# First-layer seams of a two-layer trunk: order of gates, inputs, a table load and roundings

## Chip, cores and metric

The kernel runs on one core of a Trainium2 chip. The metric is the device time of one execution in microseconds; three runs of the kernel before took 2288.21, 2284.48 and 2288.95 us (median 2288.21). A separate profiled execution gave the trace.

## What is computed

A decoder trunk of two layers over 528 tokens (16 learned meta tokens and 512 of the input), width 1024, all in float32. Each layer adds half a SwiGLU block, a mixer, and half a second SwiGLU block, each on an RMS-normalised input. Layer 0 mixes with an RWKV-7 recurrence, layer 1 with sparse attention:

```python
h = h + 0.5 * swiglu(rms_norm(h, g[0]), w_in[i, 0], w_out[i, 0])
hn = rms_norm(h, g[1])
# layer 0: six mixes of hn and its shift by one token
xx = shift(hn) - hn
xr, xw, xk, xv, xa, xg = hn + xx * mix[0..5]
r, k, v = xr @ w_r, xk @ w_k, xv @ w_v
w_log = -softplus(-(w0 + tanh(xw @ w1) @ w2)) - 0.5
a = sigmoid(a0 + (xa @ a1) @ a2)
g = sigmoid(xg @ g1) @ g2
# scan over tokens, normalisation, bonus ...
h = h + ((yn + bonus) * g) @ w_o
h = h + 0.5 * swiglu(rms_norm(h, g[2]), w_in[i, 1], w_out[i, 1])
```

The SwiGLU blocks have a hidden width of 2816.

## The kernel before, in words

**Matmuls.** Activations lie transposed, features on the 128 partitions and tokens along the free dimension, and all work is done for two ranges of tokens, A (0 to 272) and B (272 to 528). Every float32 operand of a large product is split into a rounded high part and a remainder, so that a block of weights (128x128) takes three matmuls: high by high, high by low, low by high (`mm3`). The weights come in units of 128x1024 over one DMA queue (SP); ACT rounds a unit to its high part (tile `whi`), DVE subtracts for the low part (`wlo`). `Weights.take` hands out blocks in a fixed order and, with each, has the units rounded that lie two or three ahead. `Weights.prefetch` asks for the same earlier.

**Stages of the first layer.** Feed-forward on A; projections on A; feed-forward on B, with the scan of A beside it; output projection of A, at the end of which the projections on B begin (`joined`, L1489); second feed-forward on A, with the scan of B beside it; output projection of B. The rest is the second layer and what remains of the first.

**Projections (`proj`, L882).** The normalised input and its difference to the shifted input are made per 128 features. `queue` (L917) lists 48 mixes, six of eight tiles, in the order in which they are needed. `mix` (L898) computes a mix on DVE into a tile `tb` (four buffers), takes a pair of high and low tiles from a pool of 14 (`pairs`; tile `p`) and makes a closure `make` (L906) that rounds the high part on ACT and subtracts the low part on POOL. `late` holds the closure back until the next mix has been issued; when the queue is empty it runs at once. `need` (L934) issues mixes or closures until an operand is there; `done` gives pairs back and `mixes` spends them.

`proj_steps` (L83) lists the steps: dense projections with `wk`, `wv`, `wr` in two halves of four output tiles each (kind "d"), the two low-rank first products (kind "lora", keys `lw` and `la`; `lw` ends with a tanh), the low-rank second products (kind "wa2", `decay`, L972: two banks, evacuated with a sigmoid into tile `gm`), the powers (kinds "E" and "P": exp, then sigmoid) and the eight steps of the gate's first product (`g1`). The dense results are evacuated by ACT into `BKV` and `AR`. After `g1` the gates' sigmoid goes into `R.sg` (L1042).

**Inputs of the next feed-forward.** `ahead` (L1485) first calls `norm.stat`, which does nothing when the range's rstd is there, and then walks `norm.steps` (L651): nine steps, each with an apply on DVE (into a `tb`), and, one step behind, a rounding on ACT and a subtraction on DVE into a pair. `proj` advances it once in each of the last six `g1` steps (L1038); what is left runs as the feed-forward starts.

**Statistics.** `Norm.stat` (L612) sums squares over partitions with matmuls on a tile of ones, runs eleven small DVE operations (`newton`: tile `nst`), and returns `spread` (L631), which multiplies by the identity to bring rstd to all partitions. `early` (L828) issues the statistics at item `at` of a running stage, and `spread` at an item above `at + apart`, once the planner's clock has the newton done.

**PSUM.** Four banks `acc` for large products, three `bg` for everything else, one `ry` for the scan, and for the product of `lw` (L562, L565).

**Output projection (`outproj`, L1398).** For each of eight tiles, `gate` (L1405) makes the gate's second product in a `bg` bank; DVE combines it with the scan's result, then the pair is split. Three output tiles run along with the gates (items 0 to 10 of the stage), five follow with eight items each.

**Order of work.** Each engine's order is written out by the program: a planner with a clock of modelled costs (`Clock`, `run`) weaves the chains beside the main stage. ACT, DVE and POOL run their instructions in that order.

Of the kernel before, what the change touches and what calls it, by code (L numbers as in the profile page):

```python
# [13 lines left out]
AF = mybir.ActivationFunctionType  # L14
# [10 lines left out]
A = (0, 272)  # L25
B = (272, 528)
# [12 lines left out]
NG, MIX, W0, A0, KK, KA, RK, LNG, LNB = 0, 48, 96, 104, 112, 120, 128, 136, 144  # L39
# [466 lines left out]
def trunk(ctx, tc, wall, plan, h0, vec, cstd, gqk, out, stop=None, gap=0.0, share=400.0, slack=200.0, fulls={}):  # L506
    clock = Clock()
    nc = Core(tc.nc, clock)
# [47 lines left out]
    up, down = small[:, 0:1], small[:, 1:2]  # L556
# [8 lines left out]
    def bbank(tag="bg"):  # L565
        return psum.tile([128, 512], F32, name=tag, bufs={"bg": 3, "ry": 1}[tag])
# [21 lines left out]
    class Norm:  # L588


        def __init__(self, i):
            self.gcol = NG + 8 * i
            self.ss, self.last, self.rstd = {}, {}, {}

        def add(self, d, r, lag=None):
# [16 lines left out]
        def stat(self, r, keep=True):  # L612


            if r in self.rstd:
                return None
            n = r[1] - r[0]
            q = 68 if n == 272 else 128
            nq = n // q
            p = bbank()  # L620
            for i, src in enumerate((self.ss[r], self.last[r])):
                for j in range(nq):
                    nc.tensor.matmul(p[:q, j:j + 1], src[:, j * q:j * q + q], ones[:, 0:1],
                                     start=i == j == 0, stop=i == 1, skip_group_check=True)
            st = work.tile([128, 3, 4], F32, name="nst", bufs=1)
            it = work.tile([128, 4], I32, name="nsti", bufs=1)
            x, y, a = (st[:q, j, :nq] for j in range(3))
            nc.vector.tensor_scalar(x, p[:q, :nq], EPS, None, op0=OP.add)
            newton(y, x, it[:q, :nq], a)

            def spread():  # L631
                p = bbank()
                for j in range(nq):
                    nc.tensor.matmul(p[:, j * q:j * q + q], y[:, j:j + 1].to_broadcast([q, 128]), ident[:q, :q],
                                     start=True, stop=True)
                self.rstd[r] = p
                if keep:
                    self.rstd[r] = work.tile([128, 272], F32, name="rstd", bufs=2)
                    nc.scalar.activation(self.rstd[r][:, :n], p[:, :n], AF.Copy)

            if keep:
                return spread
            W.prefetch(3 if "again" in W.kind[W.flat[W.pos][0]:W.flat[W.pos][0] + 1] else 0)
            spread()
# [183 lines left out]
    def early(main, norm, r, at=12, X=None, start=0, every=4, apart=0):  # L828


        steps = spread = None
        due = 10 ** 6
        own = Chain(None)

        def mine(f, *a):
            clock.chain = own
            x = f(*a)
            clock.chain = None
            return x

        for i, c in enumerate(main):
            if i == at:
                spread = mine(norm.stat, r)
            elif i > at + apart and spread and own.ready + gap < clock.t["tensor"]:
                spread = mine(spread)
                due = i + 3
            if X and i >= start and i > at and not spread and (own.ready - 800 <= clock.t["tensor"] or i >= due):
                steps = steps or norm.steps(X(), r)
                mine(next, steps, None)
                due = i + every  # L850
            yield c
        if spread:
            spread()
        if X:
            steps = steps or norm.steps(X(), r)
            for _ in steps:
                pass
# [24 lines left out]
    def proj(R, norm, pairs, core, ahead):  # L882
# [13 lines left out]
        xm, slot, late = {}, {}, []  # L896

        def mix(i, d):  # L898

            x = work.tile([128, 288], F32, name="tb", bufs=4)  # L900
            nc.vector.scalar_tensor_tensor(x[:, :n], xx[d // 4][:, d % 4, :n], col(MIX + 8 * i + d),
                                           hn[d][:, 1:1 + n], op0=OP.mult, op1=OP.add)
            slot[i, d] = pairs.take()
            hi, lo = (slot[i, d][1][:, j, :n] for j in range(2))

            def make():  # L906
                nc.scalar.activation(hi, x[:, :n], AF.Copy)
                nc.gpsimd.tensor_tensor(lo, x[:, :n], hi.bitcast(F32), op=OP.subtract)
                xm[i, d] = hi, lo

            if late:
                late.pop()()
            late.append(make)
            if not queue:
                late.pop()()

        queue = [(i, d) for i in (2, 1, 4, 3, 0, 5) for d in range(DT)]  # L917

        def done(i, *ds):
            for d in ds:  # L920
                pairs.give(slot.pop((i, d)))

        def mixes(k):
            while k and queue and pairs.free:
                i, d = queue.pop(0)
                if i == 2:
                    norm.apply(d, r, hn[d][:, 1:1 + n])
                    nc.vector.tensor_sub(xx[d // 4][:, d % 4, :n], hn[d][:, 0:n], hn[d][:, 1:1 + n])
                mix(i, d)
                if i == 2 and pad and d % 4 == 3:  # L930
                    nc.scalar.activation(hnlast[:, d - 3:d + 1], hn2[d // 4][:, :, n:n + 1], AF.Copy)
                k -= 1

        def need(i, d):  # L934
            while (i, d) not in xm:
                if pairs.free and queue:
                    mixes(1)
                else:
                    late.pop()()
            return xm[i, d]  # L940

        R.AR = core.tile([128, DT, 9, 2, CH], F32, name="AR")
# [2 lines left out]
        R.P = pa_[:, 0].rearrange("p m (c t) -> p m c t", t=33)  # L945
        R.a = pa_[:, 1]
        R.sg = core.tile([128, 2, 288], F32, name="sg")
        nc.gpsimd.memset(R.P[:, :, :, 0:1], 0.0)
        lslot = pairs.take()
        xw, xa = (lslot[1][:, j, :n] for j in range(2))  # L950
# [45 lines left out]
        for kind, *st in proj_steps():  # L996
            if kind == "d":
                key, g, ds = st
                if ds[0] == 0:
                    ps = [bank() for _ in range(4)]  # L1000
                x = [need(mixof[key], d) for d in ds]
                mixes(len(ds))
                for m, p in enumerate(ps, 4 * g):
                    for d in ds:
                        w = W.take(blk(key, d, m))
                        yield p[:, :n], *w, *x[d - ds[0]]
                        mm3(p[:, :n], w, x[d - ds[0]], d == 0, d == DT - 1)
                    if ds[-1] == DT - 1:
                        evac(key, m, p[:, :n])
                if g:  # L1010
                    done(mixof[key], *ds)
                    mixes(len(ds))
                yield
            elif kind == "lora":
                key, d = st
                if d == 0:
                    pl = key, bbank("ry" if key == "lw" else "bg")
                mm3(pl[1][:, :n], W.take(blk(key, d, 0)), need(mixof[key], d), d == 0, d == DT - 1)
                done(mixof[key], d)
                mixes(1)  # L1020
                if d == DT - 1:
                    lora_end(*pl)
                yield
            elif kind == "wa2":
                decay(st[0])
                if st[0] == DT - 1:
                    pairs.give(lslot)
                yield
            elif kind in "EP":
                powers(kind, st[0])  # L1030
            else:
                d = st[0]
                pg = pg or (bank(), bank())
                x = need(5, d)
                for m in range(2):
                    mm3(pg[m][:, :n], W.take(blk("g1", d, m)), x, d == 0, d == DT - 1)
                done(5, d)
                if d >= 2:  # L1038
                    next(ahead)
                if d == DT - 1:  # L1040
                    for i, k in ((0, 128), (1, 64)):
                        nc.scalar.activation(R.sg[:k, i, :n], pg[i][:k, :n], AF.Sigmoid)  # L1042
                yield
        R.have.add("all")

# [404 lines left out]
            end(m, p)  # L1450


    norms = [Norm(i) for i in range(6)]

    def first(main):

# [32 lines left out]
    def joined():  # L1489

        main = proj(RB, norms[1], pairs, core, stepsA)
        for i, c in enumerate(early(outproj(RA, pairs, norms[2]), norms[1], B, at=6, apart=4)):
            if i in (27, 31, 35):
                assert B in norms[1].rstd
                next(main)
            yield c
        yield from early(main, norms[2], A, at=100, apart=16)
# [37 lines left out]
        for _ in steps:  # L1535
            pass

    run(early(first_x(outproj(RB, pairs, norms[2], after)), norms[3], A, at=6, apart=4))
    right.close()
    xq = xa[0]  # L1540

# [456 lines left out]
```

## Time and profile before

| | |
|---|---|
| Runs | 2284.48, 2288.21, 2288.95 us |
| Profiled execution | 2284.38 us, span 2282.5 us |
| PE busy | 2217.5 us |
| DVE busy | 1662.1 us |
| ACT busy | 1274.8 us |
| POOL busy | 159.4 us |
| Mean granted PE clock | 0.995 of full |

PE is TensorE's matmuls, PEld its weight loads, DVE VectorE, ACT ScalarE, POOL GpSimd. A row of the timeline gives start and length in us, engine, line, operation, output and inputs by tile name, shape and count; the bracket behind it gives how long the engine had been idle and whose work ended that. All instructions carry line L385, that of the helper which records them, so rows are told apart by tile names: `p` are pairs (mixes, inputs, hidden tiles), `tb` the values before rounding, `gm` the decays, `sg` the gates, `nst` the statistics, `AR` and `BKV` the projections' results.

### The profile page before, as it was taken

What the parts mean: (1) busy time and instruction counts of PE and PEld (TensorE: products, weight loads), DVE (VectorE), ACT (ScalarE), POOL (GpSimd) and SP (SyncE); (2) the same over time, 40 slices, a digit from 0 to 9 for tenths busy, and PEclk for the clock granted to TensorE, in tenths of its full rate; (3) what the DMA queues carried; (4) which work ended last, traced back from release to release, by engine and by line L of the source; (5) the groups of instructions that cost most, each with busy time, mean ns of one, the idle gap of its engine ahead of it and who ended that gap; (6) DMA issues with size and microseconds to landing.
All of it is one profiled execution on the core that took longest, in us unless ns stands there. A gap on an engine that the chain in (4) does not pass through costs nothing.

```text
span 2282.5 us, 49521 instructions
## 1 busy us (share of the span) xinstructions
PE 2217.5 (97%) x20058; PEld 2151.9 (94%) x20058; DVE 1662.1 (73%) x3247; ACT 1274.8 (56%) x2186; POOL 159.4 (7%) x228
## 2 busy tenths in 40 slices
PE   8998999999999999999999999999999999999999
PEld 8998999999888999999999999899998899989999
DVE  7677777767777975686566658887657998866665
ACT  6454784475567545655444545458744657675443
POOL 0000522010052010010000000000000000000000
PEclk9999999999999999999999999999999999999999
DMA  8887757522684554255455554453454453434654
GB/s 298 282 295 253 237 200 238 188 71 86 201 306 149 172 162 130 72 190 197 166 184 165 188 171 156 166 182 133 148 178 156 158 180 117 156 104 151 190 185 139
DMA packets 115030, 405.17 MB, mean 178 GB/s; under 512 B 13024, under 2 KB 17200, under 8 KB 114800
## 3 DMA queue, kind: packets, MB, share of 16 engines
q1 hardware_dynamic: 112592, 397.07, 51.9%
q0 software_dynamic: 2208, 4.92, 0.9%
q8 instruction: 158, 2.59, 0.5%
q14 instruction: 72, 0.59, 0.1%
HBM read 380.88 MB, written 21.05 MB: 176 GB/s over the span
## 4 chain that ended last, share of the span: by engine, by line
PE 81%; DVE 9%; ACT 5%; issue 3%; DMA 1%; POOL 1%; SPq 0%; ACTq 0%; DVEq 0%; POOLq 0%
PE acc L385 69%; PE bg L385 8%; PE ry L385 4%; DVE wlo L385 3%; ACT whi L385 2%; DVE tb L385 1%; DMA wraw<-wall 1%; POOL p L385 1%; ACT p L385 1%; DVE rel L385 1%; DVE h L385 0%; ACT gm L385 0%; DVE m L385 0%; DVE pr L385 0%; ACT L385 0%
## 5 line engine op out<-in xcount | busy, mean ns | idle before, releaser
L385 ACT ACTIVATE whi<-wraw 128x1024 fp32r<-128x1024 f32 (+2 forms) x674 | 705.2, 1052 | 412.4 <-PE acc L385 247.7
L385 DVE TENSOR_TENSOR wlo<-wraw,whi 128x1024 fp32r<-128x1024 f32 (+3 forms) x628 | 767.1, 1225 | 172.0 <-ACT whi L385 162.5
L385 PE MATMUL acc<-p,whi 128*128 128x272 f32 (+1 forms) x4192 | 806.4, 291 | 24.4 <-ACT whi L385 6.2
L385 PEld LDWEIGHTS acc<-p,whi 128*128 128x128 f32 x4192 | 658.7, 190 | 34.3 <-ACT p L385 7.0
L385 PE MATMUL acc<-p,wlo 128*128 128x272 f32 (+1 forms) x2096 | 603.0, 288 | 0.4 <-DMA wlo<-lo 0.2
L385 PEld LDWEIGHTS acc<-p,wlo 128*128 128x128 f32 x2096 | 398.3, 190 | 1.1 <-DVE wlo L385 0.7
L385 PE MATMUL acc<-xa_hi,whi 128*128 128x256 f32 (+1 forms) x1088 | 311.1, 286 | 1.6 <-DVE h L385 1.6
L385 PE MATMUL acc<-xa_hi,wlo 128*128 128x256 f32 (+1 forms) x1088 | 309.4, 284 | 2.8 <-DVE wlo L385 2.7
L385 PE MATMUL acc<-xa_lo,whi 128*128 128x256 f32 (+1 forms) x1088 | 308.6, 284 | 0.0
L385 PE MATMUL acc<-hid_hi,whi 128*128 128x256 f32 (+1 forms) x880 | 252.4, 287 | 4.6 <-DVE h L385 3.4
L385 PE MATMUL acc<-hid_lo,whi 128*128 128x256 f32 (+1 forms) x880 | 248.9, 283 | 0.4 <-DVE hid_lo L385 0.4
L385 PE MATMUL acc<-hid_hi,wlo 128*128 128x256 f32 (+1 forms) x880 | 249.1, 283 | 0.0
L385 PE MATMUL acc<-xb_hi,whi 128*128 128x256 f32 x752 | 214.2, 285 | 0.0
L385 PE MATMUL acc<-xb_hi,wlo 128*128 128x256 f32 x752 | 211.4, 281 | 0.0
L385 PE MATMUL acc<-xb_lo,whi 128*128 128x256 f32 x752 | 211.4, 281 | 0.0
L385 PEld LDWEIGHTS acc<-xa_hi,wlo 128*128 128x128 f32 x1088 | 206.1, 189 | 3.9 <-DVE wlo L385 3.9
L385 PEld LDWEIGHTS acc<-xa_hi,whi 128*128 128x128 f32 x1088 | 206.2, 189 | 3.0 <-DVE h L385 1.8
L385 PEld LDWEIGHTS acc<-xa_lo,whi 128*128 128x128 f32 x1088 | 206.3, 190 | 0.0
L385 PEld LDWEIGHTS acc<-hid_hi,whi 128*128 128x128 f32 x880 | 165.8, 188 | 7.3 <-issue 4.3
L385 PEld LDWEIGHTS acc<-hid_lo,whi 128*128 128x128 f32 x880 | 166.9, 190 | 0.7 <-DVE hid_lo L385 0.6
L385 PEld LDWEIGHTS acc<-hid_hi,wlo 128*128 128x128 f32 x880 | 166.2, 189 | 0.0
L385 DVE SCALAR_TENSOR_TENSOR h<-acc,h 128x256 f32<-128x256 f32 (+1 forms) x288 | 117.0, 426 | 58.8 <-PE acc L385 58.4
(283 smaller groups left out, 3205.2 us busy)
## 6 DMA issues: line engine op xcount, KB each, us to landing
wraw<-wall SPq DMA_DIRECT2D x659, 512.0 KB, 3.6
wlo<-lo SPq DMA_DIRECT2D x46, 512.0 KB, 4.9
lo<-wlo SPq DMA_DIRECT2D x32, 512.0 KB, 4.1
wraw<-wall SPq DMA_DIRECT2D x10, 438.0 KB, 3.4
out<-h SPq DMA_DIRECT2D x8, 256.0 KB, 2.5
h<-h SPq DMA_DIRECT2D x2, 512.0 KB, 8.0
ynat<-L POOLq DMA_DIRECT2D x2, 512.0 KB, 3.8
T<-ynat POOLq DMA_DIRECT2D x2, 512.0 KB, 3.7
```

Source lines behind the costliest of these rows:

```text
L385: r = f(*args, **kw)
```

## The change

1. In the last `g1` step the two gate sigmoids are issued before the pairs are given back and before the next input step.
2. `ahead` is advanced after each step of a second half of a dense projection as soon as the queue of mixes is empty and a pair is free, and in each `g1` step when a pair is free.
3. `late` becomes first in, first out, and holds two closures instead of one; when the queue is empty all are run.
4. A sigmoid of one element is issued before the first mix of each range's projections.
5. The statistics and their spread of the norm before the second feed-forward (`norms[2]`) take the `ry` bank in place of `bg`.
6. In both output projections `early` issues the statistics at item 9 instead of 6.

```diff
-        def __init__(self, i):
-            self.gcol = NG + 8 * i
+        def __init__(self, i, tag="bg"):
+            self.gcol, self.tag = NG + 8 * i, tag
...
-            p = bbank()
+            p = bbank(self.tag)
...
-                p = bbank()
+                p = bbank(self.tag)
...
-            if late:
-                late.pop()()
             late.append(make)
-            if not queue:
-                late.pop()()
+            while len(late) > (2 if queue else 0):
+                late.pop(0)()
...
-                    late.pop()()
+                    late.pop(0)()
...
         R.sg = core.tile([128, 2, 288], F32, name="sg")
+        nc.scalar.activation(R.sg[:, 0, 0:1], down, AF.Sigmoid)
...
                     done(mixof[key], *ds)
                     mixes(len(ds))
+                    if not queue and pairs.free:
+                        next(ahead)
...
-                done(5, d)
-                if d >= 2:
-                    next(ahead)
                 if d == DT - 1:
                     for i, k in ((0, 128), (1, 64)):
                         nc.scalar.activation(R.sg[:k, i, :n], pg[i][:k, :n], AF.Sigmoid)
+                done(5, d)
+                if pairs.free:
+                    next(ahead, None)
...
-    norms = [Norm(i) for i in range(6)]
+    norms = [Norm(i, "ry" if i == 2 else "bg") for i in range(6)]
...
-        for i, c in enumerate(early(outproj(RA, pairs, norms[2]), norms[1], B, at=6, apart=4)):
+        for i, c in enumerate(early(outproj(RA, pairs, norms[2]), norms[1], B, at=9, apart=4)):
...
-    run(early(first_x(outproj(RB, pairs, norms[2], after)), norms[3], A, at=6, apart=4))
+    run(early(first_x(outproj(RB, pairs, norms[2], after)), norms[3], A, at=9, apart=4))
```

## Prediction

> **What bounds the kernel now.** I read the page first, then the time by stage, then the waits of PE in order of time, and last the rows of ACT and DVE around each wait.
>
> ```profile
> span 2282.5 us, 49521 instructions
> PE 2217.5 (97%) x20058; PEld 2151.9 (94%) x20058; DVE 1662.1 (73%) x3247; ACT 1274.8 (56%) x2186; POOL 159.4 (7%) x228
> ```
>
> PE is busy for all but 65.0 us of the span. The change adds and removes no matmul, so the only time to be had is PE's idle time, and time in which PE runs slowly. The windows below are the projections of the two ranges (212 to 326 and 636 to 740), the two output projections (597 to 636 and 1010 to 1046), and all that comes after the first layer's seams. Columns: stretch, length, busy us of PE, PEld, DVE, ACT and POOL (instructions), granted PE clock, DMA share, GB/s.
>
> ```profile
> 212.00:326.00 114.00, 101.39 (x788) 99.30 (x788) 86.73 (x137) 80.94 (x188) 47.65 (x50) 0.96 0.60 202
> ...
> 597.00:636.00 39.00, 33.32 (x257) 32.15 (x256) 30.30 (x72) 17.68 (x31) 1.67 (x2) 1.00 0.64 227
> 636.00:740.00 104.00, 95.02 (x762) 92.72 (x761) 78.57 (x124) 74.91 (x149) 42.63 (x48) 0.97 0.61 217
> ...
> 1010.00:1046.00 36.00, 32.84 (x275) 31.87 (x274) 26.61 (x67) 19.91 (x39) 0.11 (x1) 1.00 0.65 235
> 1046.00:2282.50 1236.50, 1213.47 (x9714) 1173.14 (x9713) 878.16 (x1783) 670.59 (x1086) 0.10 (x1) 1.00 0.49 161
> ```
>
> In the four stages PE idles 12.6, 5.7, 9.0 and 3.2 us: 30.5 us out of 293, against 23.0 us in the 1236 us that follow. No other engine is full there (DVE and ACT are at 71 to 78% of the projections), so these are waits in a chain, not a second bound. The timeline of PE names the waits that the change can touch; the bracket is the idle time and what ended it.
>
> ```profile
> 256.58 0.52 PE L385 MATMUL acc<-p,whi 128*128 128x272 f32 x2 [1.59 <-ACT BKV L385]
> ...
> 290.39 0.52 PE L385 MATMUL acc<-p,whi 128*128 128x272 f32 x2 [1.11 <-ACT BKV L385]
> ...
> 326.14 0.39 PE L385 MATMUL acc<-p,whi 128*128 128x256 f32 x1 [2.44 <-ACT sg L385]
> ...
> 609.50 0.36 PE L385 MATMUL bg<-p,whi 128*128 128x272 f32 x1 [1.47 <-DVE tb L385]
> ...
> 616.19 0.39 PE L385 MATMUL acc<-p,whi 128*128 128x272 f32 x1 [2.43 <-ACT p L385]
> ...
> 667.13 0.39 PE L385 MATMUL acc<-p,whi 128*128 128x256 f32 x1 [1.38 <-ACT BKV L385]
> ...
> 680.31 0.48 PE L385 MATMUL bg<-ident,nst 68*128 68x68 f32 x1 [2.46 <-ACT gm L385]
> ...
> 697.95 0.39 PE L385 MATMUL bg<-p,whi 128*128 128x256 f32 x1 [2.17 <-ACT gm L385]
> ...
> 740.87 0.40 PE L385 MATMUL acc<-p,whi 128*128 128x272 f32 x1 [2.38 <-ACT sg L385]
> ...
> 1025.95 0.39 PE L385 MATMUL acc<-p,whi 128*128 128x256 f32 x1 [0.89 <-ACT p L385]
> ```
>
> These ten make 18.3 us. Two of them are followed by a stretch in which the granted clock is a half:
>
> ```profile
> 679.69:686.52 6.83, 6.21 (x30) 6.21 (x30) 1.82 (x2) 1.57 (x5) 0.00 (x0) 0.50 0.22 77
> 741.13:744.54 3.41, 3.41 (x17) 3.41 (x17) 3.20 (x7) 2.66 (x5) 0.00 (x0) 0.50 0.00 0
> 613.76:616.19 2.43, 0.00 (x1) 0.00 (x1) 1.69 (x11) 0.48 (x2) 0.00 (x0) 1.00 1.01 325
> ...
> 299.00:318.70 19.70, 19.70 (x160) 19.70 (x159) 11.60 (x14) 19.60 (x42) 3.96 (x5) 1.00 0.48 162
> ```
>
> An equal wait at 613.76 to 616.19 did not lower it. So a wait of 2.4 us costs the clock sometimes, by where it falls.
>
> **The change part by part.**
>
> *Gate sigmoids first.* Two activations (per range) move ahead of one input step. At the end of the first projection ACT does this:
>
> ```profile
> 323.84 0.42 ACT L385 ACTIVATE p<-tb 128x256 fp32r<-128x256 f32 x1 [1.63 <-DVE tb L385]
> 324.16 1.04 ACT L385 ACTIVATE whi<-wraw 128x1024 fp32r<-128x1024 f32 x1
> 325.11 0.71 ACT L385 ACTIVATE p<-tb 128x256 fp32r<-128x256 f32 x2
> 325.72 0.65 ACT L385 ACTIVATE sg<-acc 128x272 f32<-128x272 f32 x2
> ```
>
> PE's last g1 matmul ends at 323.70 (326.14 less 2.44); the gates start 2.0 us later because three roundings of inputs and one of weights stand ahead, the first of them itself waiting 1.63 for DVE. With the inputs gone from there the gates start when PE is done. PE has two free banks to go on with, so little of the 0.65 shows; a weight rounding of 1.04 can still stand ahead. I leave 0.3 of each wait (bounds 0 and 1.0): 2.44 + 2.38 - 0.6 = 4.2 saved (2.8 to 4.8). If the wait at 740.87 goes, so should the half clock behind it: 3.41 us at a half is 1.7 (0 to 1.7).
>
> *Inputs from the last dense projection on.* The same eight applies, eight roundings and eight subtractions per range, with no statistics in them, since both ranges' rstd exist by then, and no transfer moved: the two prefetch calls ask for units that the matmuls have asked for already. Following the lists of free pairs through the steps, the queue of mixes is empty after the first `wr` step of the second half; five `wr` steps and four `g1` steps then issue all nine input steps, where before six came in `g1` and the rest after it. What is queued behind: each rounding waits for PE to have read the pair that it overwrites, and the weight roundings stand behind it on ACT. ACT has 0.10 idle in 299 to 318.7, while PE has none, so PE lives off weights rounded ahead. Four roundings of 0.42 fall into the `wr` steps, 1.7 us; the idle time just after (the 1.63 above is a part) takes them in. Cost between 0 and 1.7 per projection; I take 0.5 each, 1.0.
>
> *Sigmoid table early, statistics in the other bank.* The load exists already; it moves.
>
> ```profile
> 678.49 1.28 ACT L385 ACT_TABLE_LOAD   x1
> 679.78 0.84 ACT L385 ACTIVATE gm<-bg,vecs 128x256 f32<-128x256 f32 x2
> ...
> 219.84 0.43 ACT L385 ACTIVATE p<-tb 128x272 fp32r<-128x272 f32 x1 [6.21 <-DVE tb L385]
> 221.66 0.43 ACT L385 ACTIVATE p<-tb 128x272 fp32r<-128x272 f32 x1 [1.39 <-DVE tb L385]
> ...
> 629.06 0.42 ACT L385 ACTIVATE p<-tb 128x256 fp32r<-128x256 f32 x1 [2.21 <-DVE tb L385]
> ```
>
> Its new places are ACT's waits of 6.21 and 2.21: hidden, with the one-element activation behind it (0.43 at most, the nearest row). If that cover were gone it would cost 1.3. The next activation starts 1.29 after the load, so 1.29 is what a load costs ACT here. The Trainium skill ("ScalarE: Activation LUTs", What ACT_TABLE_LOAD costs) puts a drain of about 1.38 us on top; this trace shows none; by that rule each moved load would free 1.4 us more.
>
> At 680.31 the spread of the statistics waits for a `bg` bank that a decay's sigmoid frees. In its own `ry` bank, last read at the lora's end, well before, it waits for nothing: 2.46 saved. The spread itself takes less at full clock, as the same shape does later:
>
> ```profile
> 680.31 1.98 PE L385 MATMUL bg<-ident,nst 68*128 68x68 f32 x8 [2.46 <-ACT gm L385]
> ...
> 1027.81 1.01 PE L385 MATMUL bg<-ident,nst 68*128 68x68 f32 x8
> ```
>
> That is 0.97; and from 682.29 to 686.52 PE runs at a half, 2.1. Sum 5.5 (2.46 if the half clock comes anyway).
>
> A rule of the Trainium skill speaks against the clock terms: "TensorE: Matmul & The Clock Gate" (HAM oscillation) asks for no idle gap over about 3.4 us, so gaps of 2.4 would cost none. The rows at 679.69 and 741.13 say otherwise.
>
> *Mixes rounded two behind.* ACT takes its queue in order, and a rounding that waits for DVE holds all behind it:
>
> ```profile
> 696.17 0.42 ACT L385 ACTIVATE p<-tb 128x256 fp32r<-128x256 f32 x1 [4.34 <-DVE tb L385]
> ...
> 697.44 0.82 ACT L385 ACTIVATE gm<-bg,vecs 128x256 f32<-128x256 f32 x2
> ...
> 254.81 0.43 ACT L385 ACTIVATE p<-tb 128x272 fp32r<-128x272 f32 x1 [0.50 <-DVE tb L385]
> ...
> 256.09 1.48 ACT L385 ACTIVATE BKV<-acc 128x256 f32<-128x256 f32 x8
> ```
>
> At 697.95 the decay's sigmoids come late because of the 4.34; the rounding that stands there in the new order is of a mix issued some 40 yields earlier. 2.0 of the 2.17 go (0.8 to 2.17). At 256.58, 667.13 and 290.39 (4.08 together) the evacuations stand behind such roundings; ACT is one mix (0.9) earlier, but one weight rounding stays ahead: 2.3 (1.0 to 4.1).
>
> *Statistics at 9 for 6.* They pass the last gate. On DVE:
>
> ```profile
> 612.82 0.15 DVE L385 TENSOR_SCALAR nst<-bg 128x2 f32<-128x2 f32 x1
> ...
> 615.06 0.62 DVE L385 SCALAR_TENSOR_TENSOR tb<-AR,vecs,bg 128x256 f32<-128x256 f32 x2
> ```
>
> The Newton steps hold gate 7 up by 2.24. PE loses 1.47 and 2.43 to that gate: 3.90 idle, of which DVE's pace keeps some, so 2.2 (1.5 to 3.9). In the other range it is 0.89, of which I take 0.6, since the steps that feed the second layer start up to four yields later. The rstd is wanted 12 yields or more after its new place; the residuals queued behind the Newton steps have spare banks.
>
> Sum: 4.2 + 1.7 + 5.5 + 2.0 + 2.3 + 2.2 + 0.6 = 18.5, less 1.0: 17.5. The profiled execution took 2284.4 (span 2282.5 and 1.9 around it): 2266.9. The runs shown are 2284.48, 2288.21 and 2288.95; the profiled one is at their low end, 3.8 below the median, and I add half of that: **2268.8**.
>
> **The rivals.** (a) *Given back.* ACT and DVE are the next to be late in the projections, and what is saved in the middle (5.5 + 2.0 + 2.3) returns as waits later. Against it: 71 to 78% busy. Then 2268.8 + 9.8 = 2278.6. (b) *The half clock comes anyway*, from another cause: 1.7 + 3.1 lost, 2273.6. For it: the wait at 613.76 did not bring it; against it: both stretches stand right behind such waits. The rule of the Trainium skill named above would have it so. (c) *The table doesn't stay.* The Tanh of the lora runs between the new load and the decays; it ran without a load of its own under the old table, and no row shows it under Sigmoid's. If it swaps the table out, each projection has two loads more: 4 x 1.28, 2273.9. The Trainium skill ("ScalarE: Activation LUTs", Table sets) lists the two in one set.
>
> (d) *Slower: one mix too late.* In the first dense projection a rounding was issued two steps before its matmul, now one. If ACT reaches it only with its step, PE waits for the rounding and POOL's subtraction, 0.43 + 0.97:
>
> ```profile
> 220.35 0.97 POOL L385 TENSOR_TENSOR p<-tb,p 128x272 fp32r<-128x272 f32 x1 [214.36 <-ACT p L385]
> ```
>
> Over 2 x 8 steps 22.4 us, and the 4.3 of the rounding are not earned: 2268.8 + 26.7 = 2295.5. It decides once such a step waits over 1.0 us (16 x 1.0 against 17.5). Against it: ACT is idle before those roundings (1.39 at 221.66); DVE is late, not ACT.
>
> **How the numbers follow.** A measurement here can tell about 0.2% (4.6 us) from no change. Forecast 0.68, (a) 0.14, (b) 0.07, (c) 0.05, (d) 0.06. The bounds of the terms at their best sum to 23.1 saved (2261.3 without the added 1.9); at their worst 8.6, less 3.4 of cost, is 5.2 (2281.1 with the 1.9). Half of (a) is within 0.2%. So faster 0.87, same 0.07, slower 0.06; the range 2261 to 2281 leaves out (d), half of (a) and a tail of the forecast. The planner's later orders shift a little; that is within these bounds.
>
> **What would show it.** No wait on sg above 0.6 at the ends of the two projections; no wait of the spread near 680 and a clock of 1.00 through both places; one table load before each projection's first mix, none before its first decay; the rounding of 4.34 gone; gate 7 ahead of the Newton steps. Wrong, if as much idle stands in 212 to 326 and 597 to 740 under other names, if a weight rounding ends PE's waits in the last `wr` steps, or if new waits appear after 1046.

## The result, and the profile after

The changed kernel took 2272.7 us (median of 4 runs, 2270.34 to 2275.08), the kernel before beside it 2286.78 (4 runs): ratio 0.9941, 95% interval 0.9929 to 0.9953. That is faster by 0.6%; 2268.8 was forecast, in a range of 2261 to 2281. The profiled execution took 2272.83 us where that of before took 2284.38.

The page's first lines, and the windows by stage (columns as before):

```profile
span 2270.7 us, 49531 instructions
PE 2218.2 (98%) x20058; PEld 2152.9 (95%) x20058; DVE 1664.6 (73%) x3247; ACT 1274.3 (56%) x2188; POOL 158.6 (7%) x228
```

```profile
212.00:322.00 110.00, 101.31 (x787) 99.78 (x787) 86.47 (x135) 81.06 (x187) 45.19 (x49) 0.94 0.59 203
597.00:629.00 32.00, 30.37 (x229) 29.04 (x229) 24.20 (x62) 15.65 (x27) 0.00 (x0) 1.00 0.63 219
629.00:728.90 99.90, 95.45 (x772) 93.57 (x771) 83.08 (x132) 77.37 (x157) 44.27 (x49) 0.97 0.68 241
1001.00:1033.00 32.00, 29.65 (x251) 29.18 (x252) 22.95 (x60) 18.56 (x34) 0.11 (x1) 1.00 0.70 254
1033.00:2270.70 1237.70, 1215.00 (x9716) 1174.67 (x9715) 878.83 (x1784) 671.58 (x1088) 0.10 (x1) 1.00 0.50 161
```

PE idles 52.5 us of the span, where it idled 65.0: 12.5 less. It is busy 0.7 longer: 12.5 - 0.7 is the 11.8 that the span lost. The four stages idle 8.7, 1.6, 4.5 and 2.4 us, 17.1 together where 30.5 stood; what follows idles 22.7 (23.0 before). These windows do not hold quite the same matmuls before and after (257 and 229 in the first output projection). Cut at the same waits in both traces, the four stages idle 29.5 us before and 16.3 now, 13.1 less, and the rest of the span 0.7 more. So the idle time is won where the change lies. But in this execution the clock in the two projections is 0.94 and 0.97, no better than 0.96 and 0.97: its half-clock time was to shrink and did not. What all the runs say of the clock stands further below.

PE's timeline shows which waits went and which came:

```profile
255.22 0.52 PE L385 MATMUL acc<-p,whi 128*128 128x272 f32 x2 [1.09 <-ACT BKV L385]
285.94 0.41 PE L385 MATMUL bg<-ident,krn 96*16 96x96 f32 x3 [1.36 <-DVE krn L385]
314.97 0.52 PE L385 MATMUL acc<-p,whi 128*128 128x272 f32 x2 [0.78 <-ACT AR L385]
322.50 0.50 PE L385 MATMUL acc<-p,whi 128*128 128x256 f32 x2 [0.26 <-ACT sg L385]
607.32 0.87 PE L385 MATMUL acc<-p,whi 128*128 128x272 f32 x2 [0.86 <-ACT p L385]
629.89 0.39 PE L385 MATMUL acc<-p,whi 128*128 128x256 f32 x1 [0.42 <-POOL p L385]
631.26 0.39 PE L385 MATMUL acc<-p,wlo 128*128 128x256 f32 x1 [0.98 <-DMA wlo<-lo]
632.85 0.51 PE L385 MATMUL acc<-p,whi 128*128 128x256 f32 x2 [0.50 <-DVE h L385]
665.16 0.50 PE L385 MATMUL acc<-p,whi 128*128 128x256 f32 x2 [0.92 <-ACT BKV L385]
675.71 1.00 PE L385 MATMUL ry<-ident,nst 68*128 68x68 f32 x8
721.45 0.50 PE L385 MATMUL acc<-p,whi 128*128 128x256 f32 x2 [0.77 <-ACT AR L385]
728.89 0.52 PE L385 MATMUL acc<-p,whi 128*128 128x272 f32 x2 [0.51 <-ACT sg L385]
775.76 0.49 PE L385 MATMUL acc<-p,whi 128*128 128x272 f32 x2 [1.43 <-DVE h L385]
```

Of the ten waits that the prediction listed (18.3 us), the two on `sg` are 0.26 and 0.51; the spread at 675.71 has no bracket and takes 1.00; 697.95 and 1025.95 have no successor; the two of the output projection are one of 0.86. New are the waits on `AR`, on `krn` (a tile of the scan) and on `h`, the running sum of the layers, at 775.76; the wait on a transfer (`wlo<-lo`, low parts of weights read back from DRAM) has grown from 0.23 to 0.98. On ACT, the table loads (42 in both traces) stand where they were meant to:

```profile
623.36 1.28 ACT L385 ACT_TABLE_LOAD   x1
624.65 0.20 ACT L385 ACTIVATE sg<-small 128x1 f32<-128x1 f32 x1
...
676.40 0.82 ACT L385 ACTIVATE gm<-bg,vecs 128x256 f32<-128x256 f32 x2
```

And the half clock is at other places:

```profile
629.88:633.29 3.41, 1.92 (x11) 1.49 (x11) 2.75 (x8) 1.85 (x5) 0.00 (x0) 1.00 1.01 400
633.29:640.12 6.83, 6.48 (x29) 5.97 (x28) 6.37 (x11) 3.62 (x7) 4.28 (x5) 0.50 1.03 410
1834.79:1838.20 3.41, 1.24 (x12) 1.07 (x10) 3.38 (x7) 1.83 (x2) 0.00 (x0) 1.00 0.49 154
1838.20:1841.61 3.41, 3.41 (x16) 3.41 (x17) 3.38 (x8) 0.00 (x0) 0.00 (x0) 0.50 0.67 199
```

The second of them is in the second layer, behind a wait of 2.17 that both kernels have (at 1851.08 in the trace of before, with full clock behind it).

### The profile page after: what moved, and what is told of

Its sections match the earlier page's. It is cut to its first block, busy times and chain, and to the rows that moved or that the text cites. A ratio compares the mean times of both kernels' runs of the same rounds, so it can differ in the third digit from the quotient of the medians.

```text
span 2270.7 us, 49531 instructions
## 1 busy us (share of the span) xinstructions
PE 2218.2 (98%) x20058; PEld 2152.9 (95%) x20058; DVE 1664.6 (73%) x3247; ACT 1274.3 (56%) x2188; POOL 158.6 (7%) x228
## 4 chain that ended last, share of the span: by engine, by line
PE 58%; DVE 7%; ACT 2%; issue 1%; POOL 0%; DVEq 0%; ACTq 0%
PE acc L385 50%; PE bg L385 5%; DVE wlo L385 2%; PE ry L385 2%; ACT whi L385 1%; DVE rel L385 1%; DVE tb L385 0%; DVE m L385 0%; DVE h L385 0%; DVE pr L385 0%; DVE sc L385 0%; ACT pr L385 0%; DVE qst L385 0%; DVE BKV L385 0%; DVE pa L385 0%
```

## Experiments: the six parts one by one

The theory was the prediction's: each part removes waits of its own. The main rival was (a): what is won returns as the next wait. Six kernels have one part each put into the kernel before.

**The bank alone.**

```diff
-    norms = [Norm(i) for i in range(6)]
+    norms = [Norm(i, "ry" if i == 2 else "bg") for i in range(6)]
```

> Only the statistics of the norm before the second feed-forward move to the ry bank. Theory of the prediction (each wait is its own): the wait of 2.46 before bg<-ident,nst 68x68 near 680 is gone, and the half clock behind it too, as that wait alone brings it: 5.5 us faster (0.24%), the wait of 2.17 on gm near 698 stays. Rival (given back): PE is only early for the next late thing, so the waits on gm between 680 and 715 grow by about as much as is saved, and the time moves by less than 1.5 us. Second rival (the half clock is not that wait's own): it comes at another place, and 2.5 us is what remains.

2280.23 us, ratio 0.9969 (0.9958 to 0.9981): 4 to 10 us faster, where 5.5 was expected. Its timeline of PE at the spread and at an earlier wait, and the window behind that wait:

```profile
679.19 1.00 PE L385 MATMUL ry<-ident,nst 68*128 68x68 f32 x8
```

```profile
616.64 0.87 PE L385 MATMUL acc<-p,whi 128*128 128x272 f32 x2 [2.44 <-ACT p L385]
```

```profile
618.43:621.84 3.41, 3.41 (x17) 3.41 (x16) 2.30 (x7) 1.80 (x6) 0.00 (x0) 0.50 0.66 227
```

The spread's wait and the half clock at that place are gone. But the untouched wait at 616, behind which the clock was full in the trace of before, has half clock behind it in this one. Over all six runs the clock is better than before: 0.9958 on average, where the kernel before has 0.9943 (64 runs beside the experiments). Taken as shares of the span (an estimate) that is about 3.5 us, and with the 2.3 us that PE idles less in the trace it makes the gain.

**The table alone.**

```diff
         R.sg = core.tile([128, 2, 288], F32, name="sg")
+        nc.scalar.activation(R.sg[:, 0, 0:1], down, AF.Sigmoid)
```

> Only the one-element sigmoid before the first mix of each projection. Theory of the prediction: the load of 1.28 moves from before the first decay into ACT's wait, the Tanh brings no further load, so the number of loads stays as it is; the decay's sigmoids come 1.29 earlier and the spread's wait of 2.46 near 680 shrinks to about 1.2; 1.3 us faster, up to 4.4 if the half clock behind it goes too. If this alone ended that wait, the bank of its own would be idle. Rival: the Tanh evicts the table, one more load in each projection, no gain or up to 2.6 us slower.

2286.14 us, ratio 0.9995 (0.9986 to 1.0004): the same. The load moves and brings no other (42 again), and the waits shorten as expected:

```profile
679.93 1.11 PE L385 MATMUL bg<-ident,nst 68*128 68x68 f32 x8 [1.04 <-ACT gm L385]
698.59 0.39 PE L385 MATMUL bg<-p,whi 128*128 128x256 f32 x1 [1.13 <-ACT gm L385]
```

2.46 became 1.04, 2.17 became 1.13. PE idles 62.8 us in place of 65.0. But half clock still follows the first wait, for 10.24 us, and the mean clock of the eleven runs is 0.9936 for 0.9943, which takes back some 1.6 us by the same estimate. So the waits go and the time hardly moves; a gain of 1.3 us, as expected, is not excluded.

**Roundings two behind alone.**

```diff
-            if late:
-                late.pop()()
             late.append(make)
-            if not queue:
-                late.pop()()
+            while len(late) > (2 if queue else 0):
+                late.pop(0)()
...
-                    late.pop()()
+                    late.pop(0)()
```

> Only the roundings two behind and first in, first out. Theory of the prediction: the rounding on ACT that waited 4.34 for DVE near 696 waits no more, the wait of 2.17 on gm near 698 goes and the BKV waits (1.59, 1.11, 1.38) lose about half: 4 us faster (0.19%). Rival (given back): the start of the second projections, where the first mixes are rounded one step later, loses as much as the middle wins (PE waits on p near 630 to 640 grow by 2 us or more, half clock there): less than 1.5 us. Slower rival: 16 steps of the first dense projection wait over 1.0 us each.

2280.07 us, ratio 0.9976 (0.9965 to 0.9986): 3 to 8 us faster, where 4 was expected. The waits on `gm` at 294, 297 and 698 are gone (0.55, 0.52, 2.17 before), those on `BKV` are 1.00, none and 0.90 (1.59, 1.11, 1.38 before), and in the first dense projections no wait on a rounding or on POOL is over 0.6, apart from the first (2.14), which the kernel before has too (2.13): rival (d), which needed over 1.0 at each step, is out. It brings the wait of 1.35 on `krn` near 286, which belongs to the scan's chain; PE now reaches that chain before DVE is done with it. The waits on `sg` grow a little, to 2.63 and 2.67.

**Gate sigmoids first, alone.**

```diff
-                done(5, d)
-                if d >= 2:
-                    next(ahead)
                 if d == DT - 1:
                     for i, k in ((0, 128), (1, 64)):
                         nc.scalar.activation(R.sg[:k, i, :n], pg[i][:k, :n], AF.Sigmoid)
+                done(5, d)
+                if d >= 2:
+                    next(ahead)
```

> Only the two gate sigmoids ahead of the last input step; the inputs stay where they were. Theory of the prediction: the waits on sg at 326 and 741 (2.44 and 2.38) fall to 0.6 or less each, and the half clock of 3.41 behind the second goes: 4.2 + 1.7 = 5.9 us faster (0.26%). Rival: the roundings of the input steps that are issued in the last six g1 steps still stand ahead on ACT, so the waits only halve (2 us faster), and the inputs have to come earlier for the rest.

2285.90 us, ratio 0.9996 (0.9987 to 1.0005): the same, where 5.9 us were expected. ACT, and the wait of PE:

```profile
323.75 0.42 ACT L385 ACTIVATE p<-tb 128x256 fp32r<-128x256 f32 x1 [1.63 <-DVE tb L385]
324.07 1.04 ACT L385 ACTIVATE whi<-wraw 128x1024 fp32r<-128x1024 f32 x1
325.02 0.40 ACT L385 ACTIVATE p<-tb 128x256 fp32r<-128x256 f32 x1
325.32 0.66 ACT L385 ACTIVATE sg<-acc 128x272 f32<-128x272 f32 x2
```

```profile
325.75 0.50 PE L385 MATMUL acc<-p,whi 128*128 128x256 f32 x2 [2.16 <-ACT sg L385]
```

One rounding of 0.31 less stands ahead of the gates; the rounding that waits 1.63 for DVE and the one of weights still do, since the inputs issued in the earlier `g1` steps are unfinished. The waits stay 2.16 and 2.08.

**Inputs early, alone**, with the gates left behind the last input step.

```diff
                     mixes(len(ds))
+                    if not queue and pairs.free:
+                        next(ahead)
...
                 done(5, d)
-                if d >= 2:
-                    next(ahead)
+                if pairs.free:
+                    next(ahead, None)
```

> Only the feed-forward inputs from the last dense projection on; the gate sigmoids stay behind the input step of the last g1 step. Theory formed after the gates alone left 2.16 and 2.08: the roundings of inputs issued in the g1 steps held the sigmoids up, and once all nine input steps are out before the last g1 step, the place of the two lines is idle. Then both sg waits fall to about 0.5 or less here, the new AR waits of about 0.8 per projection come with it, the other waits of the kernel before stay: 4 to 6 us faster (0.2%). Rival (both parts are needed): sg waits of 1 us or more stay, 2 us faster or less.

2282.39 us, ratio 0.9984 (0.9975 to 0.9993): 2 to 6 us faster, where 4 to 6 were expected. The waits on `sg`, and the price on `AR`:

```profile
316.61 0.52 PE L385 MATMUL acc<-p,whi 128*128 128x272 f32 x2 [0.32 <-ACT AR L385]
324.13 0.50 PE L385 MATMUL acc<-p,whi 128*128 128x256 f32 x2 [0.27 <-ACT sg L385]
```

So part 2 removes the waits that part 1 was meant for. In the changed kernel all nine input steps are out before the last `g1` step, so it has nothing left that the gates could overtake: with only these lines put back in their old order, every engine gets the same instructions in the same order.

The part has one more price, which no wait shows. Over the first 890 matmuls of the feed-forward on B, to about 408 us, PE is busy for 83.4 to 83.6 us in all eight traces with this part, and for 82.4 to 82.5 in the four without it whose clock is full there: 0.9 more.

**Statistics at item 9 alone.**

```diff
-early(outproj(RA, pairs, norms[2]), norms[1], B, at=6, apart=4)
+early(outproj(RA, pairs, norms[2]), norms[1], B, at=9, apart=4)
...
-run(early(first_x(outproj(RB, pairs, norms[2], after)), norms[3], A, at=6, apart=4))
+run(early(first_x(outproj(RB, pairs, norms[2], after)), norms[3], A, at=9, apart=4))
```

> Only the statistics at item 9 in both output projections. Theory of the prediction: of 1.47 and 2.43 near 609 and 616 some 2.2 go, of 0.89 near 1026 about 0.6: 2.8 us faster (0.12%). Rival (given back): the wait of 1.57 on h that ends the second output projection grows by what is won there, and the start of the second projections near 630 waits for its weights' low parts from DRAM, since the stage ahead ends earlier: under 1.5 us faster.

2285.63 us, ratio 0.9995 (0.9987 to 1.0004): the same. The output projection of A, and the start of the projections of B:

```profile
611.30 0.87 PE L385 MATMUL acc<-p,whi 128*128 128x272 f32 x2 [0.86 <-ACT p L385]
...
635.92 0.39 PE L385 MATMUL acc<-p,wlo 128*128 128x256 f32 x1 [2.62 <-DMA wlo<-lo]
```

1.47 and 2.43 become 0.86, and 2.62 comes behind them: the projections begin sooner and wait for low parts of weights that are read back from DRAM. (The kernel before waits there 0.23 for the transfer, 0.73 for DVE's `h`, and 0.22 and 0.55 more further on.) In the other output projection, 0.89 goes and the wait on `h` at its end grows from 1.57 to 1.97.

What this does to the first output projection and the start of the projections of B can be read from one stretch, 469 matmuls long, from the wait of 0.74 on `tb` near 600 to the wait on `BKV` near 667. In order: the kernel before, this one, the changed kernel.

```profile
599.85:667.13 67.28, 60.05 (x470) 57.84 (x470) 55.71 (x107) 38.68 (x74) 25.75 (x30) 1.00 0.81 297
```

```profile
601.29:668.51 67.22, 61.18 (x469) 59.11 (x470) 55.66 (x107) 38.64 (x74) 25.70 (x30) 0.97 0.81 298
```

```profile
597.32:665.16 67.84, 63.36 (x470) 60.57 (x470) 55.32 (x106) 39.48 (x75) 24.80 (x29) 0.95 0.81 295
```

PE idles 7.2, 6.0 and 4.5 us in it: less each time, new waits included. But it is busy 60.05, 61.18 and 63.36 us, because its clock is lower, and the stretch is as long as before. Over all traces it takes 67.4 us on average in the six with item 9 and 67.5 in the eight with item 6.

## Experiments: what was given back

**The changed kernel, item 6 in the first output projection again.**

```diff
-early(outproj(RA, pairs, norms[2]), norms[1], B, at=9, apart=4)
+early(outproj(RA, pairs, norms[2]), norms[1], B, at=6, apart=4)
```

> The changed kernel, but the statistics in the first output projection at item 6 again. Theory (given back): 1.47 and 2.43 near 607 and 614 return in place of 0.86, and the DRAM wait near 631 goes in exchange; the time is the changed kernel's within 1.5 us. Rival (the prediction's term stands): 2.2 to 3 us slower than the changed kernel, 2275.

2271.92 us (2271.10 to 2273.44), ratio 0.9941 (0.9929 to 0.9954): the changed kernel's.

```profile
607.91 0.48 PE L385 MATMUL bg<-p,whi 128*128 128x272 f32 x2 [1.48 <-DVE tb L385]
614.61 1.07 PE L385 MATMUL acc<-p,whi 128*128 128x272 f32 x2 [2.44 <-ACT p L385]
...
636.00 0.51 PE L385 MATMUL acc<-p,whi 128*128 128x256 f32 x2 [0.43 <-DVE h L385]
```

The waits are back, the one on the transfer is gone, and the start of the projections has full clock. The half clock at 614 to 621 in this trace follows the wait of 2.44. All six traces with item 9 in that stage have half clock at their start (from 633 to 637, 3.41 to 6.83 us); none of the eight with item 6 has.

**The low parts written earlier.** To see whether the transfers are the bound there, the six low parts that the first output projection writes out for the second were chosen from its start.

```diff
-KEPT = range(4, 10)
+KEPT = range(0, 6)
```

> The changed kernel, but the six low parts that the first output projection writes to DRAM for the second are those of its units 0 to 5, not 4 to 9, so the writes lie in a stretch with DMA to spare (0.24 to 0.78) and not in the one at 0.98 ahead of the second projections. Theory: what the early end of that output projection gave back is the wait for the projections' low parts from DRAM (0.98 to 1.45 of PE idle near 631 to 633) and the half clock behind it (3.4 to 6.8 us long); both go, 3 to 4.5 us faster than the changed kernel, about 2269. Rival: the stage's start is bound by DVE (mixes and residuals), the wait on DRAM is replaced by one on DVE's p or h, and nothing is won; in the second output projection DVE has four subtractions more at its end, and the wait of 1.97 on h grows: same or 1 to 2 us slower.

2276.28 us, ratio 0.9959 (0.9946 to 0.9971): slower than the changed kernel by 3.6 of medians.

```profile
632.11 0.50 PE L385 MATMUL acc<-p,whi 128*128 128x256 f32 x2 [0.76 <-DVE h L385]
633.46 0.57 PE L385 MATMUL acc<-p,whi 128*128 128x256 f32 x2 [0.73 <-DVE h L385]
...
1032.76 0.40 PE L385 MATMUL acc<-xa_hi,whi 128*128 128x272 f32 x1 [1.09 <-DVE h L385]
1036.73 0.59 PE L385 MATMUL acc<-xa_hi,whi 128*128 128x272 f32 x1 [3.33 <-DVE h L385]
```

The rival holds. The wait on the transfer goes and DVE's work on `h` ends PE's waits in its place, with the half clock behind them as before, and the stretch shown above takes 67.8 us as in the changed kernel; at the second output projection's end DVE has four subtractions more, and 1.97 becomes 4.42, with half clock behind it from 1036.5 to 1039.9.

**The changed kernel without the early table.**

> The changed kernel without the one-element sigmoid. The table alone had shortened the spread's wait from 2.46 to 1.04 and the next decay's from 2.17 to 1.13, so it could be worth 1.3 here as well. Theory: with the bank of its own and the roundings two behind nothing waits for the first decay's sigmoids any more, the load of 1.28 stands before that decay again and PE hardly notices: within 1 us of the changed kernel. Rival: the decays behind it wait on gm by 1.0 to 1.3 us near 676 to 700 again, 1.3 us slower, or up to 4 if half clock follows.

2272.50 us (2270.56 to 2273.36), ratio 0.9941 (0.9927 to 0.9955). The load stands before the first decay again (677.10), and PE's only wait over 0.2 on a decay is

```profile
702.87 0.38 PE L385 MATMUL bg<-p,whi 128*128 128x256 f32 x1 [0.46 <-ACT gm L385]
```

With the bank and the later roundings in place, nothing waits for the first decay.

**The changed kernel, the last-but-one step of the last dense projection without an input step.**

```diff
-                    if not queue and pairs.free:
+                    if not queue and pairs.free and ds[-1] != 5:
                         next(ahead)
```

> The changed kernel, but the last-but-one step of the last dense projection issues no input step, so that no rounding that waits for DVE stands ahead of the last AR evacuations on ACT; its input step moves into a g1 step. Theory: the AR waits of 0.78 and 0.77 near 315 and 721 go and the sg waits stay at 0.5 or less: 1.5 us faster than the changed kernel (2271 beside 2272.7). Rival: ACT is full there, so what leaves AR comes back on sg, and the time is the same.

2271.72 us (2271.18 to 2273.55), ratio 0.9935 (0.9923 to 0.9948): not told apart from the changed kernel.

```profile
322.12 0.50 PE L385 MATMUL acc<-p,whi 128*128 128x256 f32 x2 [1.10 <-ACT sg L385]
...
728.11 0.52 PE L385 MATMUL acc<-p,whi 128*128 128x272 f32 x2 [1.52 <-ACT sg L385]
```

The waits of 0.78 and 0.77 on `AR` are gone; 0.26 and 0.51 on `sg` are 1.10 and 1.52. Together they made 2.32 and make 2.62. It looks as if ACT has that much to do before the feed-forward begins, and the order says only where PE waits for it.

**The changed kernel once more**, for the clock.

> The changed kernel itself once more, for the half-clock stretches. In five traces so far they begin and end on a grid of 3.41 us that stands elsewhere in each trace, and a stretch follows a grid window with about 1.7 us or more of PE idle in it. If the grid is what decides, this trace has the same waits as the first of this kernel within 0.3 us, but half clock behind others of them: the stretches at 633 and 1838 may be gone and others there, by where the grid falls. Rival (the stretches belong to the places): 213, 633 and 1838 again. Time as before, 2272.7 within 3.

2272.71 us, ratio 0.9942 (0.9929 to 0.9956). Half clock at 215, 635 and 1840, the same places. The half clock comes and goes on a grid in time, which the last section works out. It happened to stand as it did in the first trace (first stretch 1.2 us after the wait of 0.88 that starts the projection, 1.1 there), so this run does not tell the theories apart. The other traces do, below.

**Three parts alone**: inputs early, roundings two behind, the bank, with the edits shown above.

> The kernel before with three of the six parts only: inputs from the last dense projection on, roundings two behind, the bank of its own for the statistics. Left out: gate sigmoids first, the early table load, the statistics at item 9 in both output projections. Theory (these three carry the change): within 2 us of the changed kernel, 2270.5 to 2274.5, ratio to the kernel before 0.993 to 0.995; waits on sg at 0.5 or less, none of the spread near 680, none over 0.6 on gm, and 1.47 and 2.43 near 608 and 615 with no wait on DRAM behind them. Rival (each part carries its own term): the statistics at item 9 are missed with 2.8 us and the table with 1.3, 2276 to 2277.

2272.11 us (2270.95 to 2275.40), ratio 0.9939 (0.9926 to 0.9953): the whole change's, the rival's 2276 being outside. The waits on `sg` are 0.26 and 0.49 without the gates being moved. Alone the three gained 0.31, 0.24 and 0.16%; together 0.61%. No version was measurably faster than the changed kernel.

## Why the prediction was right, and where it was not

- *The sum of the waits.* Without its clock terms (1.7, 0.97 and 2.1), the prediction's 17.5 is 12.7 us of waits, against 12.5 of idle time found. The kind of gain is right, and so is its place; that the two sums agree so well is partly luck, since the misses below go both ways.
- *Gate sigmoids first (4.2).* The waits fell by 4.05, but the term was booked on the wrong edit: alone it is worth nothing that shows (2.16 and 2.08 left), and in the company of part 2 it changes no order. The step that failed is reading "three roundings and one of weights stand ahead" as removed by moving the two lines; only one of those roundings is behind them.
- *Inputs early (cost 1.0).* It earns what the other was to earn; its price, taken as 1.0, is 1.55 on `AR` in the two projections together (0.70 when it stands alone), 1.43 at 775.76, which also comes when it stands alone (1.44), and the 0.9 of busy time in the feed-forward on B.
- *The bank (5.5).* Right: 2.46, the spread at 1.00 in place of 1.98, full clock at that place, and 6.0 us of medians when it stands alone.
- *The table.* Hidden, and 42 loads as before; with the bank it earns nothing.
- *Roundings two behind (2.0 + 2.3).* 2.17 and 2.07, and 1.5 more in three waits of about 0.5 on `gm` that had not been listed; 1.36 on `krn` goes off.
- *Statistics at 9 (2.2 + 0.6).* 3.04 and 0.49 of idle time were saved there, and with new waits counted the stretch around the first still idles 2.2 us less than with item 6 put back (4.5 and 6.7): the size that was booked. But the first did not reach the end. New waits took back 0.8 of the 3.04 (1.9 where the statistics stand alone), and half clock the rest: every trace with item 9 has it at the start of the projections of B, and the stretch is no shorter on average. The prediction followed the statistics to the end of their stage and not the stage's end into the next one, where reads from DRAM and DVE are the next to be late and the short waits on them bring half clock.
- *The clock (4.8).* Right at the two places, too large in the sum. In the profiled execution half clock came at 633 and 1838, and the stretch at the first projection's start was 13.65 long for 10.24. PE's busy time, where this would show, did not fall but rose by 0.7; 4.8 and 0.7 are most of the 5.9 by which the profiled execution missed 2266.9. One execution sizes this badly, though, since half clock comes at other places in each. The mean clock is 0.9943 in the 64 runs of the kernel before beside the experiments and 0.9952 in the nine of the changed kernel: as shares of the span, an estimate, 13.1 and 10.9 us lost, so some 2.3 us won for 4.8 forecast.
- *The sum again.* 12.5 of idle time and 2.3 of clock, less the 0.9 of busy time in the feed-forward on B, make 13.9; the medians lie 14.1 apart. The trace shows small matmuls of the scan woven in there in groups of 32 in place of 64, by the planner's new order; that this is what costs the 0.9 was not tested.
- Rivals (c) and (d) did not come. Of (b) the time came (2272.7 for 2273.6), and its cause in part: the half clock left its two places and came in part elsewhere.

## What to carry to other kernels

Before booking a gain on moving an instruction forward, list what stays ahead of it on its in-order engine; the part that empties that list is the one that earns. Follow each saved microsecond through the start of the next stage: here the earlier end of a stage was spent on short waits for reads from DRAM and for the vector engine, and on the half clock behind them. And test parts alone and then the few that seem to matter together: three of six gave the whole gain.

## What the runs showed of the hardware

The half-clock stretches begin and end on a grid of 3.41 us (10.24, 6.83, 3.41 and 13.65 are multiples), which stands elsewhere in each trace. Up to the output projection the kernel with only the statistics at 9 is the kernel before, and its wait on `sg` at 326 is 2.39, before 2.44. In the trace of before, two grid windows share that wait:

```profile
321.29:324.70 3.41, 2.42 (x20) 2.20 (x18) 3.32 (x8) 1.68 (x4) 0.00 (x0) 1.00 0.81 276
324.70:328.12 3.42, 1.98 (x16) 1.98 (x17) 3.15 (x9) 2.77 (x8) 0.00 (x0) 1.00 0.79 272
328.12:331.53 3.41, 3.41 (x31) 3.41 (x30) 3.23 (x6) 2.95 (x7) 0.79 (x1) 1.00 0.56 202
```

In the other, one window holds all of it, and the next runs at a half:

```profile
322.97:326.38 3.41, 1.02 (x9) 0.81 (x8) 3.14 (x9) 2.66 (x7) 0.00 (x0) 1.00 0.82 274
326.38:329.80 3.42, 3.42 (x19) 3.42 (x18) 3.24 (x10) 2.59 (x5) 0.14 (x1) 0.50 0.44 145
```

Over the 14 traces, between 250 and 2260 us, PE waits 51 times for over 1.9 us at a stretch. By the idle time in the fullest grid window: from 1.92 to 3.12 us, half clock followed in all 24; from 1.00 to 1.87, in 2 of 27 (at 1.71, and at 1.85 before the spread's small matmuls). So a wait of this kind is followed by half clock or not by where the grid falls, and a window at a half costs about 1.7 us (half of 3.41; the windows at a half shown here hold 16 to 19 matmuls, the one at full clock above 31).

Below 1.9 us the edge is not sharp. Counted by windows at full clock, whatever waits make up their idle time, half clock followed all 24 with 1.9 us or more, 10 of the 164 with 1.0 to 1.9, and none of some 8000 with less than 1.0. Five of the ten are starts of the projections of B, with 1.5 to 1.9 us of idle time in pieces; two stand before the spread's small matmuls (1.04 with the table alone, 1.85 before). Why these and not the other 154 stays open.

The Trainium skill ("TensorE: Matmul & The Clock Gate", Part 1) has such a window, free-running and of 3413 ns; these rows agree in the length (3.41) and in that the grid stands elsewhere in each trace. Its rule of no idle gap over about 3.4 us (HAM oscillation) does not agree: 1.92 us within one window was enough.
